# Band attention: value products of four steps issued together, with six buffers of exponentials instead of three

## The chip, the cores and the metric

The kernel runs on one core of one Trainium2 chip, in float32. The metric is device time in microseconds (us) of one execution, as the median of several. Before the change three executions took 2587.08, 2587.18 and 2593.2 us, so the time before is 2587.18 us. A difference of less than about 0.3% (8 us) cannot be told from no change here.

## The reference

The program is a two-layer trunk over 1024 tokens of 1024 features. Layer 0 mixes tokens with two groups of attention heads (a latent attention and a stick-breaking attention), layer 1 with banded attention. A SwiGLU block follows each mixer and a final normalization ends the trunk. The change touches only the banded attention of layer 1, which is this, cut to what matters (16 heads of 64 features, chunks of 64 tokens, each chunk sees itself and the 8 chunks before it):

```python
def chunk_band_mixer(u, w_qkv, rel_bias, w_out):
    qkv = (u @ w_qkv).reshape(bsz, n_chunks, CHUNK, 3, C_HEADS, C_DIM)
    q, k, v = qkv[:, :, :, 0], qkv[:, :, :, 1], qkv[:, :, :, 2]
...
    scores = scores + bias.astype(jnp.float32)[None, None]
    p = jax.nn.softmax(jnp.where(valid[None, :, None, None, :], scores, -jnp.inf), axis=-1).astype(v.dtype)
    parts = [jnp.einsum('bnhqk,bnkhd->bnqhd', p[..., i * CHUNK:(i + 1) * CHUNK], v_p[:, i:i + n_chunks])
             for i in range(LEFT_CHUNKS + 1)]
    o = functools.reduce(jnp.add, parts)
    return o.reshape(bsz, seq, MIX_ODD) @ w_out
```

## The kernel before

**Tiling and steps.** Heads go in eight pairs `p`; a pair is two heads `e` of 64 features, side by side on the 128 partitions. Queries go in two halves `hf` of 512 tokens. `band_attend` (L1192) runs the steps of one pair and half: one step per block `j` of 128 keys, four for the first half, eight for the second. Because of the band a step covers 512, 384, 256 or 128 of the queries; over the layer there are 24 steps of each width, 96 in all.

**One step** has a front and a back, both made in `soft_step` (L1063). The front takes a buffer `ex` of the tag "a" (128 partitions, 2 heads by 512 queries), computes the scores of both heads into a pair of accumulator banks `z` (L1208 and L1209, weights 128 columns wide), adds the bias with VectorE into `ex` (L1210), takes the exponential in place with ScalarE (L1211), and adds `ex` to the running sum of exponentials, `b` (L1079, on GpSimd, for the last pair on VectorE). The back multiplies the exponentials with the values: `weighted` (L834, matmul at L838) does one float32 matmul per head, whose weights are only 64 columns wide, head 0 into partitions 0 to 63 of the accumulator bank `o`, head 1 into 64 to 127. In the trace each of these float32 matmuls is two records, so a step leaves four of L838. After the last step of a half, `soft_finish` (L1091) sums `b` over the partitions with two more matmuls of 64-column weights (L1095) and normalizes.

**How fronts and backs are interleaved.** `step` (L771) keeps a list of pending stages. With a lag of `LAG` = 2 the back of a step is emitted two steps after its front, before the front of that later step. Three buffers of the tag "a" serve this: two in flight and one more.

**What else runs on TensorE in that stage.** `mixer1` (L1302) weaves the steps of pair `p` with dense products as filler: the projections of the next pair's queries and keys (`band_project`, L1137) and values (`values`, L805), all through `mm3` (L284, three matmuls L287, L288, L289 with 128-column weights per tile, into the banks `mm`), and with the row maxima of the scores (`band_max`, L1168: matmuls L1182, VectorE reductions L1185; the maxima of a half are turned by a matmul at L1040). From pair 6 on little filler is left; pair 7 has the output projection of the layer (`out_half`, L421) beside its second half.

**What sets the order.** This stage is not pinned: a scheduling pass orders the instructions of each engine by its own estimate of times, subject to data and buffer dependencies. Each engine then executes its list strictly in that order. The feed-forward stages after and before it are pinned to the order of the code. Pool sizes are given in tables such as `BAND_TEMPS` (L36), tag: (buffers, columns). All DMAs are issued from SyncE.

Of the kernel before, what the change touches and what calls it, by code (L numbers as in the profile page):

```python
# [28 lines left out]
LOADS = 4  # L29
AHEAD = 2  # L30
LAG = 2
G_MIX0, G_FFN0, G_MIX1, G_FFN1, G_FIN, G_CQ, G_CKV, G_N = 0, 8, 16, 24, 32, 40, 43, 45


MIX0_TEMPS = {"a": (4, 1024), "b": (3, 1024), "c": (4, 1024), "f": (3, 512)}
BAND_TEMPS = {"a": (3, 1024), "b": (2, 1024), "f": (2, 512), "bias": (3, 1280), "t": (2, 512), "y": (4, 512)}  # L36
FFN_TEMPS = {"vr": (4, 512), "vh": (3, 512), "vl": (3, 512), "s": (4, 512), "e": (8, 512), "x": (3, 512)}

HI, LO = 4, 3
# [117 lines left out]
class Trunk:  # L157
# [724 lines left out]
    def sb_step(self, p, hf, j, proj, vt, st, o_d):  # L882
# [65 lines left out]

        idle = [lambda: None] * (LAG - 1)
        self.step(scores, *idle, weights, *idle, outputs)  # L950
# [158 lines left out]
    def mla_attend(self, p, hf, proj, vt, o_d):  # L1109
# [5 lines left out]
        for j in range(nj):  # L1115
# [15 lines left out]

            self.soft_step(2 * LAG, scores, cs, st, vt, j, j == 0, j == nj - 1, (o_d[hf], p, p == 3))
            yield 1.0 if not diag else 1.0 - 0.25 * r
# [58 lines left out]
    def band_attend(self, p, hf, proj, tk, vt, o_d):  # L1192
        nc = self.nc
        mm = nc.tensor.matmul
        qs, ks = proj
        st = {}
        order = [0, 1, 2, 3] if hf == 0 else [3, 4, 5, 6, 7, 2, 1, 0]
        for n, j in enumerate(order):
            kh, r = divmod(j, 4)
            bs = slice(r * P, (r + 1) * P)  # L1200
            i0, i1 = max(j, 4 * hf), min(j + 4, 4 * hf + 3)
            cs = slice((i0 - 4 * hf) * P, (i1 - 4 * hf + 1) * P)
            xs = slice((i0 - j) * P, (i1 - j + 1) * P)

            def scores(ex, kh=kh, bs=bs, cs=cs, xs=xs):
                z = self.banks()
                for e in range(2):
                    mm(z[:, e, cs], ks[e][kh][0][:, bs], qs[e][hf][0][:, cs], start=True, stop=False)  # L1208
                    mm(z[:, e, cs], ks[e][kh][1][0:68, bs], qs[e][hf][1][0:68, cs], start=False, stop=True)  # L1209
                nc.vector.tensor_tensor(ex[:, :, cs], z[:, :, cs], tk[:, :, xs], ALU.add)  # L1210
                nc.scalar.activation(ex[:, :, cs], ex[:, :, cs], AF.Exp)  # L1211

            self.soft_step(LAG, scores, cs, st, vt, j, n == 0, n == len(order) - 1, (o_d[hf], p, p == 7))
            yield 1.0 - 0.25 * (3 - i1 + i0)

    def with_max(self, steps, maxes, skip, every=1):
# [85 lines left out]
    def mixer1(self, u, h_d, h2_d):  # L1302
# [4 lines left out]
                                            h2_d, *e)  # L1307
        with self.phase("band", BAND_TEMPS):
            vts = [[] for _ in range(8)]
# [186 lines left out]
```

## Time and profile before

| | value |
|---|---|
| median of three executions | 2587.18 us |
| the profiled execution, its own time | 2588.75 us |
| its span, first to last instruction of the program | 2586.6 us |
| TensorE (PE) busy in the span | 2508.9 us, 97% |
| VectorE (DVE) busy | 1897.3 us, 73% |
| ScalarE (ACT) busy | 1168.5 us, 45% |
| GpSimd (POOL) busy | 515.5 us, 20% |
| mean share of the DMA engines in use | 36.9% of the span |
| granted TensorE clock (mean) | 0.992 |
| band attention, from its first step to the end of its last | about 1403 to 1875 us |

In the profile PE are matmuls and PEld the loading of their weights. "mm<-u,wh" reads "writes a tile mm from tiles u and wh". In a row of the timeline the first number is the start in us from the span's start, the second the length; "128\*64 128x512 ... x4" is four records with 128 rows by 64 columns of weights and 512 moving columns. Matmuls overlap, and their ends are modelled; so the price of one in a stream is the distance from its start to the start of the next, not its length. In a row of windows each engine's busy time in that stretch is followed by the number of its instructions. A row of groups gives the total, the mean length of one in ns, and the idle time of the engine before them.

### The profile page before, as it was taken

The page shows a single profiled execution, that of the slowest core. Times are in us where ns is not written, and L with a number is a line of the kernel's source. Part 1 is how long each engine was busy: PE and PEld are TensorE (multiplying, and loading weights), DVE is VectorE, ACT ScalarE, POOL GpSimd, SP SyncE. Part 2 cuts the span into 40 slices and gives each one's busy share as a digit, 9 for nine tenths or more (in the row PEclk, how much of TensorE's full clock was granted, in tenths as well). Part 3 has the DMA queues.
Part 4 walks back from the last instruction along what each step waited for, and adds up shares of the span by engine and source line. Part 5 has one row for each costly group of instructions (what it writes and reads, how often), then busy time and mean ns, then how long its engine had stood idle before and what let it go on. Part 6 is the DMA issues. An engine that isn't in the chain of part 4 may idle for free.

```text
span 2586.6 us, 33550 instructions
## 1 busy us (share of the span) xinstructions
PE 2508.9 (97%) x11710; PEld 1935.2 (75%) x11710; DVE 1897.3 (73%) x3074; ACT 1168.5 (45%) x2028; POOL 515.5 (20%) x489
## 2 busy tenths in 40 slices
PE   7999998999999999999999999999999999999997
PEld 6766765557778888888878777776777888888886
DVE  6888887666787666677765777777778766667776
ACT  4677676444444344443352343334445443443324
POOL 3333324663000000000031333335300000000004
PEclk9999999999999999999999999999999999999999
DMA  4221100115524343475651222222543434447661
GB/s 139 62 64 54 54 17 29 31 58 163 171 90 151 122 147 133 144 265 193 235 181 54 88 74 83 77 70 90 176 166 102 163 106 142 143 138 261 212 227 70
DMA packets 179432, 319.70 MB, mean 124 GB/s; under 512 B 20544, under 2 KB 36800, under 8 KB 179264
## 3 DMA queue, kind: packets, MB, share of 16 engines
q1 hardware_dynamic: 179264, 317.56, 36.9%
q8 instruction: 93, 1.52, 0.2%
q14 instruction: 75, 0.61, 0.1%
HBM read 222.58 MB, written 84.41 MB: 119 GB/s over the span
## 4 chain that ended last, share of the span: by engine, by line
PE 72%; DVE 9%; DMA 2%; ACT 2%; issue 1%; POOL 0%; DVEq 0%; SPq 0%; POOLq 0%; ACTq 0%
PE z L74 24%; PE mm L74 12%; PE o L74 6%; PE mm L287 6%; PE mm L289 6%; PE mm L288 6%; PE o L838 4%; DVE u L74 2%; PE z L1208 2%; PE z L1182 1%; PE z L1209 1%; PE z L1095 1%; DVE u L310 1%; PE z L1127 1%; DMA wr<-in_w_down 1%
## 5 line engine op out<-in xcount | busy, mean ns | idle before, releaser
L74 PE MATMUL z<-u,wh 128*128 128x512 f32 x976 | 302.2, 390 | 6.4 <-DVE u L74 6.4
L74 PE MATMUL z<-u,vh 128*128 128x512 f32 x976 | 301.7, 390 | 2.8 <-DVE u L74 2.8
L287 PE MATMUL mm<-u,wh 128*128 128x512 f32 x720 | 291.6, 405 | 2.9 <-DVE c L996 1.8
L289 PE MATMUL mm<-u,wl 128*128 128x512 f32 x720 | 284.0, 394 | 0.0
L288 PE MATMUL mm<-u,wh 128*128 128x512 f32 x720 | 283.9, 394 | 0.0
L255 POOL TENSOR_TENSOR wl<-wr,wh 128x512 fp32r<-128x512 f32 (+2 forms) x95 | 122.8, 1297 | 804.3 <-ACT wh L250 732.9
L74 PE MATMUL mm<-u,wh 128*128 128x512 f32 x720 | 224.6, 393 | 3.7 <-ACT wh L74 3.7
L74 PEld LDWEIGHTS z<-u,wh 128*128 128x128 f32 x976 | 183.2, 188 | 47.2 <-DVE u L74 9.4
L74 PEld LDWEIGHTS z<-u,vh 128*128 128x128 f32 x976 | 182.9, 188 | 43.0 <-ACT u L74 4.4
L74 PE MATMUL z<-u,wl 128*128 128x512 f32 x488 | 190.0, 389 | 0.5 <-DVE wl L74 0.5
L74 PE MATMUL z<-u,vl 128*128 128x512 f32 x488 | 189.9, 389 | 0.0
L287 PEld LDWEIGHTS mm<-u,wh 128*128 128x128 f32 x720 | 135.5, 188 | 63.0 <-issue 39.0
L838 PE MATMUL o<-a,u 128*64 128x512 f32 (+3 forms) x768 | 169.6, 488 | 0.2 <-ACT a L1211 0.2
L74 PEld LDWEIGHTS mm<-u,wh 128*128 128x128 f32 x720 | 135.5, 189 | 34.8 <-ACT wh L74 5.6
L289 PEld LDWEIGHTS mm<-u,wl 128*128 128x128 f32 x720 | 135.5, 188 | 32.6 <-issue 5.4
L288 PEld LDWEIGHTS mm<-u,wh 128*128 128x128 f32 x720 | 135.8, 189 | 28.6 <-issue 5.7
L74 PE MATMUL mm<-u,vh 128*128 128x512 f32 x496 | 152.7, 389 | 0.0
L255 POOL TENSOR_TENSOR u<-wr,u 128x512 fp32r<-128x512 f32 x8 | 10.9, 1373 | 667.5 <-ACT u L250 667.5
L74 PE MATMUL mm<-u,wl 128*128 128x512 f32 x360 | 141.2, 392 | 0.7 <-DVE wl L74 0.5
L1211 ACT ACTIVATE a<-a 128x1024 f32<-128x1024 f32 (+3 forms) x96 | 70.5, 738 | 145.1 <-DVE a L1210 144.9
L74 ACT CAST vh<-vr 128x512 fp32r<-128x512 f32 (+1 forms) x166 | 95.9, 577 | 81.5 <-DVE vr L74 31.5
L1079 POOL TENSOR_TENSOR b<-b,a 128x512 f32<-128x512 f32 (+3 forms) x80 | 108.0, 1350 | 114.0 <-ACT a L1211 100.0
(249 smaller groups left out, 5937.7 us busy)
## 6 DMA issues: line engine op xcount, KB each, us to landing
u<-f_t SPq DMA_DIRECT2D x144, 256.0 KB, 5.0
vr<-in_w_up SPq DMA_DIRECT2D x88, 256.0 KB, 4.4
wr<-in_w_gate SPq DMA_DIRECT2D x88, 256.0 KB, 3.6
f_t<-x SPq DMA_DIRECT2D x72, 256.0 KB, 2.0
wr<-in_w_out SPq DMA_DIRECT2D x64, 256.0 KB, 3.0
f_t<-e SPq DMA_DIRECT2D x54, 256.0 KB, 3.6
ld<-f SPq DMA_DIRECT2D x54, 256.0 KB, 5.1
h<-u SPq DMA_DIRECT2D x48, 256.0 KB, 2.5
```

What stands on the lines that cost most here:

```text
L74: return lambda *a, **k: self.tc.keep_in_program_order(f(*a, **k))
L255: self.eng(eng).tensor_tensor(lo, src, hi.bitcast(F32), ALU.subtract)
L287: mm(out, wh, xh, start=first, stop=False, skip_group_check=onto)
L288: mm(out, wh, xl, start=False, stop=False, skip_group_check=onto)
L289: mm(out, wl, xh, start=False, stop=last, skip_group_check=onto)
L310: self.eng(eng).tensor_tensor(acc, acc, sq, ALU.add)
L838: self.nc.tensor.matmul(o[rh, cs], vt[j // 4][:, j % 4, rh], w[:, e, cs], start=first, stop=last)
L1079: self.eng("dve" if dest[2] else "pool").tensor_tensor(st["esum"][:, :, cs], old[:, :, cs], ex[:, :, cs], ALU.add)
L1095: nc.tensor.matmul(den[64 * e:64 * e + 64, :], self.ones[:, 0:64], esum[:, e, :], start=True, stop=True)
L1127: mm(z[:, e, cs], kth[0:kr, bs], qh[0:kr, cs], start=True, stop=False)
L1208: mm(z[:, e, cs], ks[e][kh][0][:, bs], qs[e][hf][0][:, cs], start=True, stop=False)
L1211: nc.scalar.activation(ex[:, :, cs], ex[:, :, cs], AF.Exp)
```

## The change

In `band_attend` the lag of a step becomes `LAG + 1 + TOGETHER - 1 - n % TOGETHER`, with `TOGETHER` = 4 and `n` the number of the step in its half: 6, 5, 4 and 3 steps for the steps 0, 1, 2, 3 of a group of four. So all four backs of a group are emitted at the same place, two steps after the front of the group's last step, one behind the other. Up to six buffers of exponentials are then in flight, and `BAND_TEMPS` gives the tag "a" six buffers instead of three (4 KB per partition each, so 12 KB more). The room comes from an argument of the program's constructor, `dynamic_dma_scratch_size=1024`, which was left at its default before. The latent attention of layer 0, which uses the same `soft_step` with a lag of 4 (L1132), is not touched.

```diff
 LAG = 2
+
+TOGETHER = 4
...
-BAND_TEMPS = {"a": (3, 1024), "b": (2, 1024), "f": (2, 512), "bias": (3, 1280), "t": (2, 512), "y": (4, 512)}
+BAND_TEMPS = {"a": (6, 1024), "b": (2, 1024), "f": (2, 512), "bias": (3, 1280), "t": (2, 512), "y": (4, 512)}
...
-            self.soft_step(LAG, scores, cs, st, vt, j, n == 0, n == len(order) - 1, (o_d[hf], p, p == 7))
+
+            self.soft_step(LAG + 1 + TOGETHER - 1 - n % TOGETHER, scores, cs, st, vt, j, n == 0, n == len(order) - 1, (o_d[hf], p, p == 7))
...
-    nc = _bacc.Bacc("TRN2", target_bir_lowering=False, num_devices=1)
+    nc = _bacc.Bacc("TRN2", target_bir_lowering=False, num_devices=1, dynamic_dma_scratch_size=1024)
```

The program's order changes on all engines between the first and the last band step, and nowhere else. On TensorE, around one step of 512 queries of pair 3, second half, the order before is this (o is the output accumulator, a the exponentials, z the scores, mm the bank of a dense product):

```order
L288 MATMUL mm_13800<-wl_13779,u_11468 128x256
L289 MATMUL mm_13800<-wh_13778,u_11469 128x256
L838 MATMUL o_13741<-a_13698,u_13356 64x512 x2
L1208 MATMUL z_13813<-u_13094,u_13217 128x256
L1209 MATMUL z_13813<-u_13095,y_13218 128x256
L1208 MATMUL z_13813<-u_13099,u_13223 128x256
L1209 MATMUL z_13813<-u_13100,u_13224 128x256
L287 MATMUL mm_13800<-wh_13778,u_11468 128x256
```

and after the change, on TensorE, where the four steps of the first half of pair 3 are multiplied with the values (the changed file's line numbers are higher by two or three):

```order
L290 MATMUL mm_13705<-u_11793,wh_13652 128x512
L291 MATMUL mm_13705<-u_11792,wl_13653 128x512
L840 MATMUL o_13721<-a_13448,u_12800 64x512 x2
L840 MATMUL o_13721<-a_13490,u_12800 64x384 x2
L840 MATMUL o_13721<-a_13559,u_12800 64x256 x2
L840 MATMUL o_13721<-a_13587,u_12800 64x128 x2
L1097 MATMUL z_13730<-b_13498,ones 64x512 x2
L1210 MATMUL z_13742<-u_13087,u_13214 128x384
```

A step's two value matmuls stood alone between matmuls of 128-column weights; now eight of them, and here the two of the sum as well, stand in one row. Counted over the whole stage, the unbroken runs of 64-column matmuls (L838 and L1095) go from 107 to 37. Most of the 37 hold four whole steps. Where filler is short (pairs 6 and 7) the scheduler breaks some up again, and it parts the two heads of a step from each other at six steps, where before it did so at four.

On VectorE the first three bias additions of a half stand like this before (pair 3, second half; a_13631, a_13698 and a_13744 are three successive buffers of exponentials):

```order
L1210 TENSOR_TENSOR a_13631<-z_13632,bias_13311 128x1024
L1146 SCALAR_TENSOR_TENSOR t_13711<-mm_13663,u_11648 128x512
L1210 TENSOR_TENSOR a_13698<-z_13699,bias_13311 128x1024
L1099 SCALAR_TENSOR_TENSOR z_13687<-z_13687,f_13690 128x512
L255 TENSOR_TENSOR u_13713<-t_13711,u_13713 64x512
L1100 SCALAR_TENSOR_TENSOR f_13690<-z_13687,f_13690 128x512
L255 TENSOR_TENSOR u_13719<-t_13711,u_13719 64x512
L1101 TENSOR_TENSOR f_13691<-o_13559,f_13690 128x512
L255 TENSOR_TENSOR wl_13791<-wr_13788,wh_13790 128x512
L1210 TENSOR_TENSOR a_13744<-z_13745,bias_13311 128x2x384
L1146 SCALAR_TENSOR_TENSOR t_13762<-mm_13725,u_11888 128x512
```

and like this after, at the same place (a_13741 is the seventh buffer taken since a_13448, the first of the row above on TensorE):

```order
L1212 TENSOR_TENSOR a_13624<-z_13625,bias_13304 128x1024
L1212 TENSOR_TENSOR a_13678<-z_13679,bias_13304 128x1024
L257 TENSOR_TENSOR u_13699<-t_13691,u_13699 64x512
L257 TENSOR_TENSOR wl_13788<-wr_13785,wh_13787 128x512
L1212 TENSOR_TENSOR a_13741<-z_13742,bias_13304 128x2x384
L1101 SCALAR_TENSOR_TENSOR z_13730<-z_13730,f_13733 128x512
L1102 SCALAR_TENSOR_TENSOR f_13733<-z_13730,f_13733 128x512
L1148 SCALAR_TENSOR_TENSOR t_13759<-mm_13705,u_11888 128x512
```

The additions themselves keep their number and shape. The normalization of the first half (three operations, L1099 to L1101 before) moves behind the third addition of the next half, since its sum is now taken at the end of the row of eight.

## The prediction

> **What bounds the kernel now.** I read the page first, then the windows of the stage that changes, then its timeline on TensorE record by record, and the waits last.
>
> ```profile
> span 2586.6 us, 33550 instructions
> PE 2508.9 (97%) x11710; PEld 1935.2 (75%) x11710; DVE 1897.3 (73%) x3074; ACT 1168.5 (45%) x2028; POOL 515.5 (20%) x489
> ```
>
> Whole-span shares are averages over stages. The windows of the band stage (first row all of it, then one head pair's period in two parts, then the time of pairs 6 and 7 with little filler, then the start of what follows; columns: length, busy time of PE, PEld, DVE, ACT, POOL with their counts, granted clock, DMA share, GB/s) say it more sharply:
>
> ```profile
> 1403.00:1875.00 472.00, 469.14 (x2467) 332.96 (x2465) 353.06 (x730) 190.91 (x332) 182.96 (x173) 1.00 0.30 92
> 1482.97:1517.06 34.09, 33.95 (x207) 25.27 (x206) 25.08 (x42) 14.91 (x28) 16.88 (x17) 1.00 0.25 77
> 1517.06:1542.21 25.15, 25.15 (x120) 17.56 (x119) 18.82 (x50) 8.21 (x13) 5.13 (x6) 1.00 0.28 86
> 1766.00:1815.00 49.00, 47.68 (x225) 28.60 (x223) 41.20 (x87) 23.27 (x39) 27.22 (x23) 1.00 0.31 90
> 1875.00:1900.00 25.00, 25.00 (x109) 20.19 (x108) 19.70 (x31) 11.56 (x20) 0.00 (x0) 1.00 0.72 240
> ```
>
> TensorE is busy 469.14 of 472.00 us at clock 1.00, so this stage lasts as long as its stream of matmuls. What shortens that stream shortens the kernel, until another engine is late. A pair's period is 34.09 + 25.15 = 59.24 us, in which VectorE works 25.08 + 18.82 = 43.90 us (74%).
>
> But a busy PE can be an idle array. The timeline shows it in the distances between starts. Around one step of 512 queries:
>
> ```profile
> 1490.76 0.39 PE L287 MATMUL mm<-u,wh 128*128 128x512 f32 x1
> 1490.99 0.39 PE L288 MATMUL mm<-u,wh 128*128 128x512 f32 x1
> 1491.21 0.39 PE L289 MATMUL mm<-u,wl 128*128 128x512 f32 x1
> 1491.53 1.08 PE L838 MATMUL o<-a,u 128*64 128x512 f32 x4
> 1492.54 0.44 PE L1208 MATMUL z<-u,u 128*128 128x384 f32 x1
> 1492.82 0.34 PE L1209 MATMUL z<-u,y 68*128 68x384 f32 x1
> 1493.00 0.34 PE L1208 MATMUL z<-u,u 128*128 128x384 f32 x1
> ```
>
> A dense matmul follows the last after 0.23 us; the value product starts 0.32 after it: entering costs 0.09. The first score matmul afterwards takes 0.28 to the next start, the second 0.18: leaving costs 0.10. Steps of the other widths, each with the start that follows it:
>
> ```profile
> 1500.78 0.87 PE L838 MATMUL o<-a,u 128*64 128x384 f32 x4
> 1501.58 0.33 PE L1208 MATMUL z<-u,u 128*128 128x128 f32 x1
> 1501.74 0.28 PE L1209 MATMUL z<-u,y 68*128 68x128 f32 x1
> 1501.86 0.27 PE L1208 MATMUL z<-u,u 128*128 128x128 f32 x1
> ...
> 1515.58 0.65 PE L838 MATMUL o<-a,u 128*64 128x256 f32 x4
> 1516.16 0.50 PE L287 MATMUL mm<-u,wh 128*128 128x512 f32 x1
> ...
> 1508.69 0.44 PE L838 MATMUL o<-a,u 128*64 128x128 f32 x4
> 1509.06 0.39 PE L1208 MATMUL z<-u,u 128*128 128x256 f32 x1
> ```
>
> The steps of 512, 384, 256 and 128 queries take 1.01, 0.80, 0.58 and 0.37 us: 0.213 per 128 queries plus 0.157 that each lone step pays whatever its width. Where a 128-wide matmul follows, leaving costs only 0.05 (0.16 to the next start, against 0.12 for the one after it).
>
> **The change, part by part.**
>
> *Fewer runs.* Does the 0.157 fall due once a run, or once a step? The old program has one place that tells: its last two band steps (256 and 128 queries, eight records) and the two sums stand in one row.
>
> ```profile
> 1873.51 0.87 PE L838 MATMUL o<-a,u 128*64 128x256 f32 x8
> 1874.21 1.03 PE L1095 MATMUL z<-b,ones 128*64 128x512 f32 x4
> 1875.17 0.50 PE L287 MATMUL mm<-u,wh 128*128 128x512 f32 x1
> ```
>
> 896 queries in all took 1875.17 - 1873.51 = 1.66 us. Once a run: 7 x 0.213 + 0.157 = 1.65. Once a step: 7 x 0.213 + 3 x 0.157 = 1.96. So it is once a run, and so are entering and leaving. By count 107 runs become 37: 70 are removed, some 19 of which are followed by 128-wide matmuls. One is worth 0.157 + 0.09 + (51 x 0.10 + 19 x 0.05) / 70 = 0.157 + 0.09 + 0.087 = 0.334 us, all 70 together 23.4 us. In one pair's period 13 runs become 3, so 59.24 becomes about 55.9 us.
>
> The Trainium skill holds a rule that speaks against this: "TensorE: Matmul & The Clock Gate", in "Part 3: Packing small matmuls — row/col tiling", says that weight loads overlap matmuls in flight only where the row group differs, and the value products all use the same 128 rows; by it every step in a row would still pay its 0.157, and only entering and leaving would be saved. The row of 1.66 us disagrees with that; the case is a rival below.
>
> *Heads parted.* Two heads of a step run side by side only while they stand together:
>
> ```profile
> 1762.28 1.07 PE L838 MATMUL o<-a,u 128*64 128x512 f32 x2
> 1763.28 0.44 PE L1182 MATMUL z<-u,u 128*128 128x128 f32 x2
> ```
>
> One head alone took 1.00 us, as much as the two together (1.01). So a parted step costs its 0.213 per 128 queries a second time. Before, steps of 256, 128, 512 and 384 are parted (10 x 0.213 = 2.13 us), after it three of 384, two of 512 and one of 256 (19 x 0.213 = 4.05). This costs 1.9 us. If the first head of the next step can run beside the one left over, it is less: between 0 and 1.9. The trace has no such place; I take 1.9, the price of the row above.
>
> *Later backs, six buffers.* The seventh buffer waits until the first step's back is done. In the VectorE order above, a_13741 is that buffer; its scores z_13742 stand behind the row of eight on TensorE anyway, so the addition waits for its scores, not longer for its buffer. Queued behind it are the normalization and the copy of a dense bank (L1148). Who waits for those? TensorE goes on into the other dense bank first and needs the copied one only after it, so it doesn't. The nearest row of such waits:
>
> ```profile
> DVE a L1210 <- PE z L1209: 50.7, 43, 4.2
> ```
>
> VectorE already waits 50.7 us here for scores, up to 4.2 at a time, and TensorE still runs without gaps. Cost 0, covered by TensorE's filler; without filler (pairs 6 and 7) it is counted next.
>
> *Who is late next.* VectorE must do the same 43.90 us in 55.9, 79%. That fits, but not everywhere. In the stretch with the row maxima it has no room:
>
> ```profile
> 1529.00:1533.00 4.00, 4.00 (x21) 2.86 (x21) 3.94 (x12) 1.73 (x3) 0.05 (x1) 1.00 0.45 130
> 1533.00:1537.00 4.00, 4.00 (x22) 2.10 (x21) 3.47 (x14) 1.37 (x3) 1.67 (x2) 1.00 0.21 66
> 1537.00:1541.00 4.00, 4.00 (x20) 3.30 (x20) 3.94 (x14) 0.80 (x2) 0.42 (x1) 1.00 0.29 68
> ```
>
> VectorE works 11.35 of these 12 us. Three runs leave the stretch (1.0 us), which leaves 11.0: 0.35 short in each of some six periods, 2.1 us, if the scheduler hadn't moved anything ahead. In pairs 6 and 7 TensorE idles already (47.68 of 49.00 above), once for a sum of exponentials:
>
> ```profile
> PE z L1095 <- DVE b L1079: 1.4, 1, 1.4
> ```
>
> There the count of runs falls little, and what it gives (0.6 us) may be waited away; or that wait may go (1.4 us gained). Together between 2.7 lost and 1.4 gained; I take 1.5 lost, nearer to the first, whose row is the fuller one.
>
> *The smaller scratch.* The page's queues:
>
> ```profile
> q1 hardware_dynamic: 179264, 317.56, 36.9%
> q8 instruction: 93, 1.52, 0.2%
> q14 instruction: 75, 0.61, 0.1%
> ```
>
> All data moves on the queue whose kind is hardware_dynamic, issued by SyncE; none is issued by GpSimd. I take 0. The Trainium skill ("SBUF — State Buffer", "SBUF size: 192, 224, or 256?") calls this scratch the descriptor ring of DMAs described in software, of which no run here shows one; by that page the price is 0 as well. If the hardware queue did use it, loads would come late throughout; that is part of the slower case.
>
> **Sum.** 23.4 - 1.9 - 1.5 = 20.0 us. The profiled execution's span of 2586.6 becomes 2566.6, its own time of 2588.75 becomes 2568.75; against the median of 2587.18 the forecast is **2567.2 us**, 0.8% faster. About 0.3% (8 us) is what a measurement can tell from no change.
>
> **Rivals.**
>
> *Every step still pays inside its row.* Then 70 x (0.09 + 0.087) = 12.4 is saved, less 3.4: 9.0 us, 2578.2. For it stands the rule named above; against it the 1.66 us. Chance 0.06.
>
> *VectorE becomes the bound in each period.* If the row maxima's stretch loses all three runs' gain (6 us) and what waits in the sparse pairs doubles the loss, some 8 of the 20 us go: 2575. For it: 11.35 of 12 us. Against it: after that stretch VectorE has slack, and two score banks and two dense banks let it lag. Chance 0.10.
>
> *What follows takes it back.* If the feed-forward stage waits for its weights, its start doesn't move: 2587, no change. For it: DMA share 0.72 in the last window. Against it: TensorE is busy 25.00 of 25.00 us there, and its loads are issued relative to the same work as before. Chance 0.05.
>
> *Slower: each row waits for its last exponential.* TensorE works strictly in order, so a row of eight placed too soon after its last scores stops everything, where before a wait held up one step's product. The chain to wait for is one addition and one exponential, at their longest 1.22 + 1.06 us:
>
> ```profile
> L1210 DVE TENSOR_TENSOR a<-z,bias 128x1024 f32<-128x1024 f32 x24 | 29.3, 1224 | 16.6 <-PE z L1209 11.4 <-issue 4.4 <-POOL u L1156 0.8
> L1211 ACT ACTIVATE a<-a 128x1024 f32<-128x1024 f32 x24 | 25.4, 1059 | 29.6 <-DVE a L1210 29.4
> ```
>
> 24 rows x 2.28 = 55 us against 21.5 saved: 33 us slower, 2620. It decides from 0.9 us per row on. Against it: the lag keeps two further fronts between the last scores and the row, and in the order some 9 dense matmuls (2 us) follow even those. Chance 0.04, a starved DMA queue included.
>
> **How the numbers follow.** The forecast has 0.75. Faster by over 0.3%: 0.75 + 0.10 and the first rival, which lies just past the bound (0.06): 0.91. Same 0.05, slower 0.04. The range goes from 2562 (no loss to VectorE, the parted heads free, the 1.4 us wait gone: 23.4 + 1.4 = 24.8) to 2578 (the first two rivals within it).
>
> **What would show it.** Right: the band stage about 452 us long instead of 472; L838 in rows of 16 records; a block of 512, 384, 256, 128 and the sums of 512 taking 14 x 0.213 + 0.157 = 3.14 us; a period of about 55.9. If starts inside a row lie 0.157 further apart at each step, the first rival holds. If PE idles before L838 for an exponential, the slower one. If the period exceeds 57 with VectorE busy throughout, the second. If the stage shrinks and the total doesn't, the third. Wrong altogether: a total above 2579.

## The result and the profile after

| | before | after |
|---|---|---|
| median of six executions, us | 2588.89 | 2574.98 |
| ratio to before, 95% interval | | 0.9944 [0.9932, 0.9956] |
| span of the profiled execution, us | 2586.6 | 2571.9 |
| banded stage, first row-maximum matmul to last sum matmul | 478.4 | 463.8 |
| what lies after it | 712.0 | 713.8 |
| runs of 64-column matmuls in the stage | 107 | 37 |

The change gains 0.56%. In the spans that is 14.7 us; the stage accounts for 14.6 of them. What lies ahead of it takes 1.9 us less and what lies after it 1.8 us more, in instructions that are the same. The forecast was 20.0. From the page of the kernel after, the span and the first lines of the engines:

```profile
span 2571.9 us, 33553 instructions
PE 2483.8 (97%) x11710; PEld 1938.0 (75%) x11710; DVE 1885.4 (73%) x3074; ACT 1170.4 (46%) x2028; POOL 518.1 (20%) x489
q1 hardware_dynamic: 179264, 317.56, 37.0%
```

TensorE has as many records as before and is busy 25.1 us less; the data queue moved the same bytes. The windows of the kernel after: most of the stage, and one pair's period in its two parts (columns as in the prediction):

```profile
1403.00:1858.00 455.00, 446.06 (x2457) 337.24 (x2458) 341.06 (x729) 192.86 (x332) 184.71 (x173) 1.00 0.31 95
1477.48:1510.28 32.80, 31.51 (x203) 25.01 (x203) 22.61 (x42) 15.14 (x28) 15.21 (x14) 1.00 0.22 74
1510.28:1534.78 24.50, 24.50 (x123) 18.57 (x124) 19.73 (x51) 8.32 (x13) 6.90 (x9) 1.00 0.32 95
```

A period went from 59.24 to 32.80 + 24.50 = 57.30 us, where 55.9 was forecast. The part with the row maxima is full (24.50 of 24.50). The other part is not: TensorE is busy 31.51 of 32.80, a gap of 1.29 us that was not there before (33.95 of 34.09).

The price of the rows is as worked out. TensorE's timeline of the kernel after, a whole first half of pair 3 with its sums:

```profile
1539.88 0.39 PE L291 MATMUL mm<-u,wl 128*128 128x512 f32 x1
1540.19 2.38 PE L840 MATMUL o<-a,u 128*64 128x512 f32 x16
1542.40 1.03 PE L1097 MATMUL z<-b,ones 128*64 128x512 f32 x4
1543.36 0.44 PE L1210 MATMUL z<-u,u 128*128 128x384 f32 x1
1543.64 0.34 PE L1211 MATMUL z<-u,y 68*128 68x384 f32 x1
```

From 1540.19 to 1543.36 are 3.17 us, 0.03 over the 3.14 named in the prediction. Entering (0.31 where the next dense matmul follows after 0.23) and leaving (0.28 against 0.18) are paid once.

So where is the gap? The waits of the kernel after, in the stage:

```profile
DVE a L1212 <- PE z L1211: 70.1, 38, 3.4
PE z L1210 <- DVE a L1212: 7.2, 6, 1.2
```

The second row is new: six times, once a period, TensorE stops for a score bank that VectorE's bias addition frees late. Each stop puts 1.36 us more between two matmuls than is usual for their shapes (1.20 us of it are in the row), 8.2 us in all six. This is the VectorE timeline of the kernel after behind the row shown above, at one of the stops:

```profile
1544.44 0.96 DVE L1212 TENSOR_TENSOR a<-z,bias 128x768 f32<-128x768 f32 x1 [3.34 <-PE z L1211]
...
1546.64 0.68 DVE L1148 SCALAR_TENSOR_TENSOR t<-mm,u 128x512 f32<-128x512 f32 x1
...
1547.84 0.98 DVE L257 TENSOR_TENSOR wl<-wr,wh 128x512 fp32r<-128x512 f32 x1
1548.85 0.69 DVE L257 TENSOR_TENSOR u<-t,u 64x512 fp32r<-64x512 f32 x1
1549.57 0.69 DVE L1212 TENSOR_TENSOR a<-z,bias 128x512 f32<-128x512 f32 x1
1551.60 1.31 DVE L257 TENSOR_TENSOR u<-t,u 64x512 fp32r<-64x512 f32 x1 [1.34 <-ACT u L252]
1552.94 0.42 DVE L1212 TENSOR_TENSOR a<-z,bias 128x256 f32<-128x256 f32 x1
```

and this is TensorE's timeline there:

```profile
1551.93 0.28 PE L291 MATMUL mm<-wh,u 128*128 128x256 f32 x1
1553.42 0.44 PE L1210 MATMUL z<-u,u 128*128 128x384 f32 x1 [1.20 <-DVE a L1212]
```

The bias additions of the third, fourth and fifth step of the second half start at 1544.44, 1549.57 and 1552.94; the scores of the sixth step (1553.42) need the bank of the fifth. From the third addition to the sixth step's scores it is 8.98 us. The same place before, VectorE and then TensorE:

```profile
1554.62 0.95 DVE L1210 TENSOR_TENSOR a<-z,bias 128x768 f32<-128x768 f32 x1
...
1556.98 1.98 DVE L255 TENSOR_TENSOR wl<-wr,wh 128x512 fp32r<-128x512 f32 x1 [0.82 <-ACT wh L250]
1558.99 0.69 DVE L255 TENSOR_TENSOR u<-t,u 64x512 fp32r<-64x512 f32 x1
1559.71 0.69 DVE L1210 TENSOR_TENSOR a<-z,bias 128x512 f32<-128x512 f32 x1
1561.84 1.21 DVE L255 TENSOR_TENSOR u<-t,u 64x512 fp32r<-64x512 f32 x1 [1.43 <-ACT u L250]
1563.08 0.42 DVE L1210 TENSOR_TENSOR a<-z,bias 128x256 f32<-128x256 f32 x1
```

```profile
1560.03 0.87 PE L838 MATMUL o<-a,u 128*64 128x384 f32 x4
...
1562.76 0.65 PE L838 MATMUL o<-a,u 128*64 128x256 f32 x4
1563.55 0.19 PEld L1208 LDWEIGHTS z<-u,u 128*128 128x128 f32 x1 [0.59 <-DVE a L1210]
1563.56 0.44 PE L1208 MATMUL z<-u,u 128*128 128x384 f32 x1
```

From 1554.62 to 1563.56 are 8.94 us, nearly the same. VectorE was as slow before, and TensorE waited for it even then, a little: the fifth addition ended at 1563.50 and the scores started 0.06 us behind it, as they do after the change (1553.36 and 1553.42). The value product of 256 queries ahead of them has 0.80 us to the next start, where the prediction's row of that width has 0.58. These 0.21 us are lost in five of the six periods, 1.1 us in all; the matmuls have no row for them in the list of waits, because it is the loading of the weights that is noted as waiting (PEld). Two value products, of 0.80 and 0.58 us, stood in this stretch on TensorE. They were the cover of this sequence, already a little too short, and the change took them away. That is what the two profiles suggest; what makes the sequence 9 us long is for the experiments.

### The profile page after: what moved, and what is told of

It reads as the page before. It is cut to its first block, busy times and chain, and to the rows that moved or that the text cites. A ratio compares the mean times of both kernels' runs of the same rounds, so it can differ in the third digit from the quotient of the medians.

```text
span 2571.9 us, 33553 instructions
## 1 busy us (share of the span) xinstructions
PE 2483.8 (97%) x11710; PEld 1938.0 (75%) x11710; DVE 1885.4 (73%) x3074; ACT 1170.4 (46%) x2028; POOL 518.1 (20%) x489
## 4 chain that ended last, share of the span: by engine, by line
PE 71%; DVE 10%; DMA 2%; issue 1%; ACT 1%; POOL 0%; DVEq 0%; SPq 0%; POOLq 0%; ACTq 0%
PE z L76 24%; PE mm L76 12%; PE o L76 6%; PE mm L289 5%; PE mm L290 5%; PE mm L291 5%; PE o L840 4%; DVE u L76 2%; PE z L1210 1%; PE z L1184 1%; PE z L1211 1%; DVE u L312 1%; PE z L1097 1%; PE z L1129 1%; DMA wr<-in_w_down 1%
## 5 line engine op out<-in xcount | busy, mean ns | idle before, releaser
L840 PE MATMUL o<-a,u 128*64 128x512 f32 (+3 forms) x768 | 155.3, 476 | 0.0
L1212 DVE TENSOR_TENSOR a<-z,bias 128x1024 f32<-128x1024 f32 (+3 forms) x96 | 78.1, 822 | 75.8 <-PE z L1211 70.1
```

The lines of the kernel that those rows point to most:

```text
L840: self.nc.tensor.matmul(o[rh, cs], vt[j // 4][:, j % 4, rh], w[:, e, cs], start=first, stop=last)
```

## The experiments

Each ratio is to the kernel before, run beside it, with its 95% interval. "Stage" is the stage's length as in the table; a stop is the distance it adds between two matmuls. The first four were set up with a narrower theory R: the row of ten holds back the third step's scores, so VectorE idles (3.34 us above), is late afterwards, and so TensorE stops. Rival B: the six buffers, or the smaller scratch, cost something by themselves. Rival C: the missing 5 us are the granted clock, whose mean over an execution was 0.990 in some.

**The buffers alone** (six buffers and the small scratch, the lag left at 2; each engine's order is that of before):

```diff
-            self.soft_step(LAG + 1 + TOGETHER - 1 - n % TOGETHER, scores, cs, st, vt, j, n == 0, n == len(order) - 1, (o_d[hf], p, p == 7))
+            self.soft_step(LAG, scores, cs, st, vt, j, n == 0, n == len(order) - 1, (o_d[hf], p, p == 7))
```

> Six buffers of exponentials and the smaller scratch, but the old lag of 2, so that the order of all engines stays that of before (107 runs of 64-column matmuls). Theory R (the gain is the removed runs, and what the forecast missed is a stop of TensorE behind each row of ten): no change, ratio 0.999 to 1.001, no stop. Rival B (buffers, addresses or the scratch cost something by themselves and ate the missing 5 us): ratio 1.002 or more.

Measured: 0.9979 [0.9969, 0.9989], 2585.54 us; stage 477.1, 1.4 less than before. The buffers cost nothing, B falls, and they are not what the change gains. The rest of this kernel's lead, which R had not expected either, lies outside the stage, in instructions that are the same; the last experiment comes back to it.

**One step later** (every lag one more, seven buffers, a scratch of 256):

```diff
-LAG + 1 + TOGETHER - 1 - n % TOGETHER
+LAG + 2 + TOGETHER - 1 - n % TOGETHER
```

> As after, but each row of four steps is issued one step later (seven buffers, scratch of 256), so that the scores of the seventh step stand ahead of the row and not behind it; 31 runs. Theory R: VectorE has its addition and the dense bank's copy done before the row, so its wait of 3.34 us at the row no longer makes it late, and the six stops of about 1.3 us at the sixth step's successor go: after minus 8 us, minus 6 x 0.334 = 2 us for six fewer runs, so ratio about 0.990 to the kernel before (2564 us). Rival B (a longer lag, more buffers cost): no better than after, ratio 0.994 or above. Rival C (the missing 5 us are the clock, which ran at 0.990 in some executions): only the 2 us, ratio 0.9935.

Measured: 0.9922 [0.9909, 0.9935], 2572.52 us; 31 runs, stage 459.3. The stop fell to 0.36 us. New ones came before the row-maximum matmuls (L1184), 0.35 and 0.43 in each of five periods. Summed over the stage, the distances between matmuls exceed the usual ones for their shapes by about 17.6 us here, 17.8 in the changed kernel and 10.1 before (64-column runs and the step out of them aside; the sums hold to about 0.5 us, by what one calls usual). So the lost time is that of the change, and the shorter stage comes from fewer runs. The ratio lies between the theories' numbers: the stop can be moved away, but not every wait with it.

**The first half's sums one step later** (only the two matmuls of L1097 and the normalization behind them, in pairs 0 to 6):

```diff
-            if last:
+            if last and not split:
                 self.soft_finish(st["o"], st["esum"], *dest)
...
+        def finish():
+            self.soft_finish(st["o"], st["esum"], *dest)
...
-        self.step(front, *[lambda: None] * (lag - 1), back)
+        self.step(front, *[lambda: None] * (lag - 1), back, *([finish] if split and last else []))
```

> As after, but the sums and the normalization of a first half (pairs 0 to 6) are issued one step later than its row of eight, so that the row is 1 us shorter, the next scores come 1 us earlier, and VectorE copies the dense bank before it normalizes; 40 runs instead of 37, and slightly more parted heads (4.9 instead of 4.05 us). Theory R: the stop shrinks from 1.3 us to at most 0.3: 6 to 8 us gained, 1.9 lost: ratio about 0.992 (2569 us). Rival C (clock): 2 us slower than after, ratio 0.995.

Measured: 0.9905 [0.9892, 0.9919], 2568.28 us; 40 runs, stage 459.3. The stop fell from 1.36 to 0.36, at a granted clock of 1.00 in the stage as in both kernels, so C falls. Of the versions that compute everything this has the lowest ratio; its stage is as long as that of the version one step later, so what it has over that one lies outside the stage. Its TensorE timeline in the same stretch:

```profile
1541.83 1.08 PE L1100 MATMUL z<-b,ones 128*64 128x512 f32 x4
...
1548.05 0.44 PE L1213 MATMUL z<-u,u 128*128 128x384 f32 x1 [0.20 <-DVE a L1215]
```

The sums' run (1.01 us) now stands between the third and the sixth step. R had forecast the number for another reason; that TensorE simply has 1.0 us more to do there is as good an account, and the next experiment decides.

**Rows of four only in the second half:**

```diff
-LAG + 1 + TOGETHER - 1 - n % TOGETHER
+LAG + 1 + TOGETHER - 1 - n % TOGETHER if hf else LAG
```

> Rows of four steps in the second halves alone; the first half's four steps keep the lag of 2. 65 runs, parted heads 6.8 us instead of 2.1. Theory R: 42 x 0.334 - 4.7 = 9.3 us saved and no stop of over 0.5 us in a second half, since no row of ten stands ahead of its scores: ratio 0.9964 (2580 us). If instead the stops belong to the rows of the second half, they stay (8 us): ratio 0.9995.

Measured: 0.9994 [0.9984, 1.0004], 2590.03 us; 65 runs, stage 478.7. No row of ten stands ahead of the second half here, yet at the sixth step's scores:

```profile
1502.82 0.45 PE L1210 MATMUL z<-u,u 128*128 128x384 f32 x1 [0.96 <-DVE a L1212]
```

This stop adds 1.12 to 1.70 us, once a period. So R falls: the row of ten is not what makes VectorE late. What this kernel shares with the changed one is that no value product stands between the third and the sixth step. The lost time, counted as above, is 21.4 us, and with 42 runs fewer nothing was gained.

Theory V took R's place: the cover was removed, and VectorE is late because the normalization of the first half stands ahead of the fourth addition. **Two instructions of the normalization left out in first halves, after and before.** Both kernels leave out a part of the computation; the edit is the same in both:

```diff
+        if refine:
             nc.vector.scalar_tensor_tensor(den, den, -1.0, r, ALU.mult, ALU.mult)
             nc.vector.scalar_tensor_tensor(r, den, 2.0, r, ALU.add, ALU.mult)
```

> The changed kernel without the two VectorE instructions that refine the reciprocal of the softmax sums, for the first half of every pair (this part of the computation is left out; 8 x 2 instructions of 128x512, 0.60 to 0.73 us each). Theory V (the stop was covered before): in every period VectorE's addition for the fourth step of the second half starts 1.6 us after its scores are there, because the normalization of the first half stands ahead of it, and from that addition to the sixth step's scores it is 3.85 us in both kernels (1559.71 to 1563.56 before, 1549.57 to 1553.42 after). TensorE's own work between the two score steps shrank by the value products that moved away. Without the two instructions the addition starts 1.3 us earlier, so the stop of 1.36 us falls to 0.1 or less, six times; four runs fewer at the stage's end give 1.3 us more: the stage is 463.8 - 7.4 - 1.3 = 455 us, the ratio to before 0.991. Rival D (the stop is set by the rotation of the score banks or by ScalarE's order, not by when VectorE gets to the addition): the stop stays at 1.2 to 1.4 us, the stage 462.5, the ratio 0.994. Rival W (the stop goes, but VectorE's earlier finish only moves the wait to another place): the stage 460 or more with new stops of the same sum.

> The kernel before with the same two VectorE instructions left out for first halves (part of the computation is left out). Its partner is the changed kernel with the same edit. Theory V: before, TensorE's own work reaches the sixth step's scores (1563.56) just as VectorE has freed the bank (1563.50), so an earlier VectorE gains nothing there: the stage stays at 478.4 within 1.5 us, the ratio 0.999 to 1.000. A rival by which VectorE's work in the stage costs time by itself in both kernels: 6 x 1.3 = 8 us less here too, the ratio 0.997.

Measured, changed kernel: 0.9954 [0.9941, 0.9968], 2576.68 us, stage 463.3. The stop stayed at 1.37 us in all six periods. Kernel before: 1.0013 [1.0001, 1.0025], 2592.48 us, stage 482.7; a period took 59.07 instead of 59.24 us, and the 4.3 us more of the stage lie at pairs 6 and 7 (why was not pursued). The two instructions cost nothing to speak of in a period of the changed kernel (57.27 without them, 57.30 with them), and V is wrong in its second half: there the normalization does not set when the fourth addition comes. In the kernel before they cost the 0.17 us, about the small wait at the sixth step's scores, which is gone without them:

```profile
1562.45 0.65 PE L838 MATMUL o<-a,u 128*64 128x256 f32 x4
1563.03 0.44 PE L1209 MATMUL z<-u,u 128*128 128x384 f32 x1
```

The value product has its 0.58 us to the next start again. V had expected no gain at all in a period here. What sets the time after the change is seen in the changed kernel without the two instructions, VectorE, GpSimd and TensorE:

```profile
1541.91 0.96 DVE L1213 TENSOR_TENSOR a<-z,bias 128x768 f32<-128x768 f32 x1 [3.33 <-PE z L1212]
...
1544.52 1.79 DVE L257 TENSOR_TENSOR wl<-wr,wh 128x512 fp32r<-128x512 f32 x1
1546.34 0.69 DVE L257 TENSOR_TENSOR u<-t,u 64x512 fp32r<-64x512 f32 x1
1547.06 0.69 DVE L1213 TENSOR_TENSOR a<-z,bias 128x512 f32<-128x512 f32 x1
1549.09 1.30 DVE L257 TENSOR_TENSOR u<-t,u 64x512 fp32r<-64x512 f32 x1 [1.34 <-ACT u L252]
```

```profile
1543.89 1.86 POOL L1081 TENSOR_TENSOR b<-b,a 128x768 f32<-128x768 f32 x1 [2.82 <-ACT a L1214]
1548.56 1.28 POOL L1081 TENSOR_TENSOR b<-b,a 128x512 f32<-128x512 f32 x1 [2.80 <-PE z L1185]
```

```profile
1550.90 0.44 PE L1211 MATMUL z<-u,u 128*128 128x384 f32 x1 [1.21 <-DVE a L1213]
```

VectorE came to the subtraction `wl<-wr,wh` 2.61 us after the third addition instead of 3.40, and was held in it: it ended at 1546.31, 0.56 us after GpSimd's addition to the sums (1543.89 + 1.86 = 1545.75), and the second subtraction at 1550.39, 0.55 after GpSimd's second one. From the third addition (1541.91) to the sixth step's scores it is 8.99 us, as with the whole normalization. In the changed kernel GpSimd's two additions stand here:

```profile
1546.42 1.85 POOL L1081 TENSOR_TENSOR b<-b,a 128x768 f32<-128x768 f32 x1 [2.83 <-ACT a L1213]
...
1551.07 1.29 POOL L1081 TENSOR_TENSOR b<-b,a 128x512 f32<-128x512 f32 x1 [2.80 <-PE z L1184]
```

They end at 1548.27 and 1552.36; VectorE's subtractions of 0.98 and 1.31 us end at 1548.82 and 1552.91, both 0.55 later. Theory P: GpSimd's additions hold VectorE's subtractions up. **Those two additions left out (the result then lacks two steps in its sums), and held back:**

```diff
+                if add:
+                    self.eng("dve" if dest[2] else "pool").tensor_tensor(st["esum"][:, :, cs], old[:, :, cs],
+                                                                         ex[:, :, cs], ALU.add)
...
+            self.soft_step(LAG + 1 + TOGETHER - 1 - n % TOGETHER, scores, cs, st, vt, j, n == 0, n == len(order) - 1, (o_d[hf], p, p == 7), hf == 0 or n not in (2, 3))
```

> The changed kernel without GpSimd's additions of the third and the fourth step's exponentials to the sums of the second half (128x768 and 128x512, left out in all pairs, so those steps are missing from the denominators); the order on TensorE and ScalarE is that of the changed kernel. Theory P: while GpSimd adds, VectorE's subtractions from SBUF to SBUF stand still: the one at 1547.84 ended 0.55 us after GpSimd's addition of 1546.42 to 1548.27, the one at 1551.60 ended 0.55 us after that of 1551.07 to 1552.36, and without the normalization they ended 0.56 and 0.55 us after them as well. Without the additions the first subtraction ends 0.4 us earlier and the second takes 0.7 instead of 1.3 us: the addition that frees the score bank is 0.9 to 1.0 us earlier, the stop of 1.36 us falls to 0.35 to 0.45, six times 0.95 = 5.7 us: the stage 458, the ratio to before 0.992. Rival N (only VectorE and ScalarE make the 9 us between the third and the sixth step, GpSimd's rows only lie beside them): the stop stays at 1.36 us, the stage 463 to 464, the ratio 0.9945.

```diff
+                add = lambda old=old: eng.tensor_tensor(st["esum"][:, :, cs], old[:, :, cs], ex[:, :, cs], ALU.add)
+                if when == "hold":
+                    st.setdefault("held", []).append(add)
+                else:
+                    add()
+                    if when == "free":
+                        for f in st["held"]:
+                            f()
...
+            self.soft_step(LAG + 1 + TOGETHER - 1 - n % TOGETHER, scores, cs, st, vt, j, n == 0, n == len(order) - 1, (o_d[hf], p, p == 7), hf and {2: "hold", 3: "hold", 5: "free"}.get(n))
```

> The changed kernel with the same two additions of GpSimd not left out but held back until after the sixth step's addition is due. The order on TensorE and ScalarE is that of the changed kernel. Theory P: the stop falls to 0.35 to 0.45 us as when they are left out; the additions then hold off VectorE's casts and subtractions in the stretch of the row maxima behind it, by up to 1.3 + 1.9 us a period, of which TensorE may feel none (458) or half (463 or more): the stage 458 to 463, the ratio 0.992 to 0.994. Rival N: the stop stays, the stage 464, the ratio 0.9945.

Measured, left out: 0.9927 [0.9914, 0.9941], 2567.47 us, stage 457.9, the stop 0.44 us in all six periods. Its VectorE rows and the stop:

```profile
1542.74 0.68 DVE L257 TENSOR_TENSOR wl<-wr,wh 128x512 fp32r<-128x512 f32 x1
...
1546.19 0.69 DVE L257 TENSOR_TENSOR u<-t,u 64x512 fp32r<-64x512 f32 x1 [1.34 <-ACT u L252]
```

```profile
1547.39 0.44 PE L1211 MATMUL z<-u,u 128*128 128x384 f32 x1 [0.28 <-DVE a L1213]
```

0.68 and 0.69 us instead of 0.98 and 1.31, and the stop 0.92 shorter: P's numbers, N falls. Held back: 0.9935 [0.9923, 0.9948], 2571.51 us, stage 459.6, the stop 0.44 to 0.46. The additions cost nothing in the row maxima, whose stretch stayed full and as long:

```profile
1479.71:1511.50 31.79, 31.50 (x203) 24.98 (x202) 21.54 (x42) 15.14 (x28) 15.16 (x14) 1.00 0.23 78
1511.50:1535.96 24.46, 24.46 (x123) 18.56 (x124) 19.70 (x51) 8.32 (x14) 6.88 (x9) 1.00 0.31 94
```

Against leaving them out it loses 1.7 us, at the end of the stage (two waits of 0.96 and 0.79 us around pairs 6 and 7).

**Later sums and held additions together** (the two edits above in one kernel):

> The version with the first half's sums one step later (2568.3, stage 459.3, a stop of 0.36 us left in each period), and GpSimd's two additions held back as well. Theory P: the remaining stops go too, 6 x 0.36 = 2.2 us: the stage 457, the ratio 0.990; if the held additions are paid in the row maxima: 459 to 461, the ratio 0.991.

Measured: 0.9930 [0.9917, 0.9942], 2569.82 us, stage 459.6. A miss: the stops of 0.36 us stayed, six times. With the sums later, GpSimd's two additions are not what these stops hang on; what is, stays open.

**Two steps together instead of four:**

```diff
-TOGETHER = 4
+TOGETHER = 2
```

> Only the number of steps taken together is 2 instead of 4. In the order of the instructions TensorE then has 69 runs of 64-column matmuls in the stage instead of 107 before and 37 after, but 13.8 us of matmuls whose other head does not stand beside them, instead of 2.1 and 4.1. If a run costs 0.334 us and a parted head its whole length: 38 x 0.334 = 12.7 us gained, 11.7 us lost, so 1 us faster, less what the stops take: the stage 477 to 481, the ratio 0.9985 to 1.001. If parted heads cost nothing and only runs count: the stage 466, the ratio 0.995. If neither runs nor parted heads count but the six buffers do: the ratio 0.998, as with the buffers alone.

Measured: 0.9978 [0.9967, 0.9989], 2582.54 us, stage 471.5: 6.9 us less than before, where 1 was expected. The price of a parted head was too high. TensorE's timeline of this kernel:

```profile
1414.29 1.07 PE L840 MATMUL o<-a,u 128*64 128x512 f32 x4
1415.30 0.62 PE L1184 MATMUL z<-u,u 128*128 128x384 f32 x2
```

The first row (it names the shape of its first record) is two records of 512 and two of 384, a head left over from one step beside the next step's first. Together they took 1.01 us, as much as the 512 alone. All 64-column runs of the stage took 84.6 us in this kernel (from a run's start to that of what follows), and 84.7 before, of which 1.1 are the small waits, so 83.6. 38 runs fewer are 38 x 0.157 = 6.0 less; so parting cost 84.6 - 83.6 + 6.0 = 7.0 instead of the 11.7 that counting widths gave. The same account of the changed kernel, 74.6 - 83.6 + 70 x 0.157, gives 2.0.

**The same grouping in layer 0's latent attention as well**, on top of the later sums:

```diff
-MIX0_TEMPS = {"a": (4, 1024)
+MIX0_TEMPS = {"a": (6, 1024)
...
-            self.soft_step(2 * LAG, scores, cs, st, vt, j, j == 0, j == nj - 1, (o_d[hf], p, p == 3))
+            self.soft_step(LAG + 1 + TOGETHER - 1 - j % TOGETHER, scores, cs, st, vt, j, j == 0, j == nj - 1, (o_d[hf], p, p == 3))
```

> The version with the first half's sums one step later, and the value products of the latent attention of layer 0 taken by four as well, with six exponential buffers there instead of four. In the order of the instructions TensorE has 35 runs in that stage instead of 49, and 10.65 us of parted heads instead of 15.34. By the price of the banded stage: 14 x 0.334 = 4.7 us and 4.7 us, together 9.4 us less than the version with later sums (2568.3): 2559 us, a ratio to before of 0.988. If layer 0 is bound by VectorE or ScalarE there, or stops of TensorE take it back as in the banded stage: 2563 to 2568, a ratio of 0.990.

Measured: 0.9948 [0.9934, 0.9963], 2575.21 us: slower than the later sums alone, by 6.9 us in the times and by 11 in the ratios. The stage of layer 0, from its first scores to its last sums, took 228.4 us instead of 222.7. The windows of this kernel and then of its partner, and two waits that only this kernel has:

```profile
520.00:620.00 100.00, 92.15 (x388) 59.00 (x388) 75.75 (x81) 44.46 (x70) 50.56 (x36) 0.95 0.27 88
```

```profile
520.00:620.00 100.00, 96.88 (x435) 64.11 (x434) 69.65 (x88) 48.75 (x78) 55.39 (x39) 1.00 0.31 101
```

```profile
PE z L1132 <- DVE f L1105: 3.1, 1, 3.1
PE z L1042 <- DVE maxes L1040: 2.5, 1, 2.5
```

TensorE is busy 92.15 of 100 us instead of 96.88 and waits for VectorE; the granted clock is 0.95 there instead of 1.00. Over the whole of that stage the clock is 0.96 against 0.98. The kernel before, at 0.96 as well and with the partner's order there, took 225.8 us for it; so by an estimate from these three profiles some 2.6 of the 5.7 us come with the new order and the rest with the clock. Other lags were not tried.

**The scratch alone**, in the kernel before:

```diff
-    nc = _bacc.Bacc("TRN2", target_bir_lowering=False, num_devices=1)
+    nc = _bacc.Bacc("TRN2", target_bir_lowering=False, num_devices=1, dynamic_dma_scratch_size=1024)
```

> The kernel before with the dynamic DMAs' scratch cut to 1 KB and nothing else: every instruction is that of before. If the smaller scratch costs something where transfers are dense: slower than before, 1.001 or more, most of it outside the band. If it costs nothing: 0.999 to 1.001. If the gain of 3 to 5 us that the six buffers alone showed comes with the scratch and not with the buffers: 0.998.

Measured: 1.0011 [1.0000, 1.0023], 2592.63 us, stage 478.4. The scratch costs nothing that can be told and gains nothing, so the lead of the buffers alone outside the stage does not come from it. Layer 0's latent attention, the same instructions in all of them, took 225.8 us in the profile before, 222.7 after, 222.0 with the buffers alone and 223.7 with the scratch alone. The granted clock there was 0.96, 0.98, 0.99 and 0.97 in this order: the lower the clock, the longer. Differences of a few us between kernels that are not in the stage are of this kind; why the clock differs from one profile to the next stays open, and stages are compared here by their own length.

## Why the prediction was right, and where its terms were off

**The total.** 2575 lies inside the range because the range made room for the first two rivals; the forecast's own sum was some 5 us too high, by one term that it had put at nothing.

**Fewer runs: right.** 107 became 37, and a row costs its 0.157 once; with 70 x 0.334 = 23.4 us for this the sum below closes to 0.2 us, within the 0.5 of its counting. The first rival (every step still pays) is dead by the row of 3.17 us; by it that row would take 14 x 0.213 + 5 x 0.157 = 3.77. The rule of the Trainium skill that stood for it ("TensorE: Matmul & The Clock Gate", "Part 3: Packing small matmuls — row/col tiling") has no effect that shows here: the steps in a row share their 128 rows and follow one another without the 0.157.

**Heads parted: right in size.** 2.0 us by the records, where 1.9 was taken. That a head left over can run beside the next step's first, the reason for the lower bound, is so as well; it shows with two steps together, where parting cost 7.0 instead of 11.7.

**Later backs, six buffers: the step that failed.** "Cost 0, covered by TensorE's filler" was the term, because "TensorE goes on into the other dense bank first". It costs 6 x 1.36 = 8.2 us, 7.1 more than the small waits of before. The buffers indeed cost nothing, and the addition waits for its scores, as said. But the question was put to the dense bank, while the wait is for a score bank two steps later. Cover was counted as if it stayed: the value products of the third and fourth step were part of what TensorE had to do meanwhile, and they are what the change moves away. Nor did TensorE run without gaps before: at the sixth step's scores it stood 0.21 us for this very bank, which the row at 1562.76 shows by its 0.80 us to the next start. The cover had no room to lose.

**Who is late next: the right engine, the wrong place.** The second rival's time (2575) came out, its mechanism not; that they agree is chance. A period of 57.30 passes the 57 that was named as its sign, but VectorE is not busy throughout: 22.61 + 19.73 = 42.34 us of it. The stretch of the row maxima, with its 11.35 of 12 us, stayed free of stops. VectorE is late where it is used less (22.61 of 32.80 us), since there it waits in turn: for a ScalarE cast queued behind an exponential (1.34 us), and for GpSimd. Shown by experiment is GpSimd's part: without its two additions 0.92 of the 1.36 us go. That the moved value products were the cover is shown less directly: by the 8.94 and 8.98 us, at whose end TensorE waits in both kernels, by the stop that stays without a row of ten ahead, and by the sums' run that removes 1.0 us of it when it is put in.

**The scratch and what follows: right.** No effect of the scratch that can be told, and what follows kept its length to 1.8 us. No matmul of a row waited for its last exponential.

**The sum.** The lost time grew by 17.8 - 10.1 - 1.1 (the small waits of before) = 6.6 us. 23.4 - 2.0 - 6.6 = 14.8 us; the stage measured 14.6. The forecast's 20.0 had 1.9 and 1.5 in the places of 2.0 and 6.6.

## What to carry to other kernels

When instructions are moved together on the busiest engine, look at what they stood in front of: for each place that loses one, compare when the engine would now arrive with when the buffer it needs is freed. A busy share says little about that; an engine at 70% can be late if it waits in a chain. And before a wait is charged to an engine's load, look at the ends of its long instructions: if they keep a fixed distance to the end of another engine's, leave out that one, not the load.

## What the runs showed of the hardware

- VectorE's subtraction with both inputs in SBUF (0.68 us alone), begun while GpSimd adds in SBUF, is held until GpSimd has done. It ended 0.55 or 0.56 us after GpSimd's addition in all four cases above, up to 1.1 us late, and by the records in all 21 of the changed kernel's stage 0.54 to 0.55 us after. VectorE's operation with one input from an accumulator bank (L1148, 0.68 us at 1546.64) ran at full pace under the same addition. The Trainium skill ("SBUF — State Buffer", "Who interferes with whom") says that a VectorE instruction with two SBUF inputs contends with a GpSimd instruction that reads SBUF, and one with at most one such input, outside the modes in which VectorE uses two ports, does not; the subtractions agree with the first half and L1148 with the second.
- One SBUF input alone is no safe sign, though: VectorE's cast `wh<-wr` (L254, 0.41 us at its shortest) was held as well. All twelve that began under such an addition in the changed kernel's stage ended 0.28 us after it, the longest after 1.35 us. Whether they ran in one of those modes no run here shows.
- Two 64-column matmuls in different column halves run side by side whatever step they belong to and even with different widths: 512 and 384 together took 1.01 us.
